# Waits tile by tile, gate functions behind the cells, and attention output reloaded earlier, in a hybrid mLSTM and attention layer

## The chip, the cores and the metric

The kernel runs on one core of one Trainium2 chip. The metric is the device time of one execution in microseconds (us). A core has a matrix engine (PE, with its weight loads PEld), a vector engine (DVE), a scalar engine (ACT), a general engine (POOL), and a sync engine (SP) that mostly issues transfers between the chip's memory (DRAM) and the core's own memory (SBUF). The engines run side by side, each through its own list in order, and wait for each other through semaphores. PE writes to eight banks of a small memory (PSUM), which DVE and ACT empty.

## The reference, cut to what matters

One layer works on 640 tokens (512 latent tokens and 128 context tokens) of width 1024:

```python
hh = rmsnorm(x, g[0]) * (1 + m[1]) + m[0];  x = x + 0.5 * m[2] * swiglu(hh, w1, w3, w2)
hh = rmsnorm(x, g[1]) * (1 + m[4]) + m[3];  x = x + m[5] * token_mixer(hh)
hh = rmsnorm(x, g[2]) * (1 + m[7]) + m[6];  x = x + 0.5 * m[8] * swiglu(hh, w1, w3, w2)
# token_mixer:
att = diff_attention(...)            # 8 heads: softmax_0 - lam * softmax_1, times values
hm  = rmsnorm(h_forward + h_backward) * sigmoid(mo)      # 4 heads of a chunked mLSTM
y   = sigmoid(gm) * (hm @ w_br_m) + sigmoid(gd) * (att @ w_br_d);   out = y @ w_out
```

The modulation m is `silu(c) @ w_ada + b`, 9216 numbers for each of two conditions. The mLSTM runs over five chunks of 128 tokens (four latent, one context) forward and backward; every step multiplies the chunk's masked scores with its values, adds the query times the state C, and updates C. All of it is float32: a product is made of three products of split halves (high times high, high times low, low times high).

## The kernel before, in words

**Tiles and stages.** Features lie on the 128 partitions. The stages follow one another: first feed-forward (to about 480 us), projections and the eight attention heads (to about 1085), the four mLSTM heads (to about 1250), the two branch products and the output product (to about 1440), second feed-forward. A weight granule of 1 MB is loaded into one of two `raw` buffers, copied by ACT to its high half (`wH`, L123) and subtracted by DVE to its low half (`wL`); two granules are held split. A unit is 24 matrix products of one granule into one PSUM bank, with an evacuation behind it.

**Filling.** `Fill` holds a list of granules of projections that nothing waits for at once (gates, values, queries of later heads). Between the steps of a head, `fill.slot` puts some of their units into PE's list, so that PE has work while DVE and ACT make the softmax or the next state. `prefetch` splits the next granule ahead.

**The order of the work.** PE's list is in the order in which the code is written (`keep_in_program_order` in `mm` and `tr`). The lists of the other engines are made by a planner, which simulates the program and takes what is ready first, in the order of the code where several are ready. `tc.issue_after(ins)` adds an edge that puts the instructions of a block behind `ins` in their engine's list, without a wait for its end.

**Memory and waits.** Tiles come from pools; a pool's tiles with the same tag share its buffers. When a pool takes over memory of a pool that was closed, the default is that its tiles wait for the whole old pool; with `reuse_waits="tile"` each waits only for the old tiles whose memory it covers. Some pools of the first and last stages have this before the change, the pools of attention (`att`, `ps2`, `ps2s`), of mLSTM (`ml`, `ps3`) and of the branch products (`ps4`, `tmp`, `yy`, `gate`, `out`) do not.

**Around the hand-over.** The last attention head ends with `finish_norm`, the rest of the fill list, and `finish` (L1324 on), which turns its output into `aT` through two banks and stores it to `aT_dram`. Then the pools of the mLSTM stage open, `csil` and `mask` are loaded, and `Memory.load` (L1580) loads the values (`va`, L1583) and the row maxima (`P`, L1588) of the first head and adds the mask to P on DVE; `load_c` loads both states C. `prep` makes a chunk's token-major keys and scores, `cell` one step in one direction, `gate` (L1662) the output gate `so` by two ACT functions (L1665, L1666), `finish` (L1676) the norm, the gate and the turn back. While head h runs its ten cells, the five preparations of head h+1 and the five finishes of head h-1 are spread over them (`later`).

**Columns.** `Columns` makes the last 24 tiles of the modulation (L683): 512 KB of `w_ada` per tile, two passes of DVE over 1024 columns, one per condition. In the mLSTM stage and beside the branch products their data lie in the `raw` buffers, which the weights use too. `attended` reloads the attention output for the branch product, three pairs at a time through `raw`, and splits it; `drain_beside_columns` runs the branch units, with one column tile to two units.

## Time and profile before

| what | value |
|---|---|
| median of three runs | 1884.49 us (1882.04 to 1887.07) |
| the profiled execution's own time | 1881.62 us |
| its span, first to last instruction | 1879.8 us |
| granted PE clock, mean over the span | 0.986 |
| busy: PE, DVE, ACT, POOL | 97%, 69%, 45%, 2% |
| transfers | 299.82 MB, mean 159 GB/s |

The profile is one execution. Busy is the share of the span in which an engine worked on something; waits are idle time just before an instruction, put down to what came last ("ACT aT L1331" is the instruction of line 1331 that writes the tile aT). "issue" is idle time for which the profile shows no releaser. PEclk is the share of full speed that PE's clock was granted. A row of the timeline has start, duration, engine, line, operation, out<-in, shapes, count, and in brackets the idle time before it. SPq and POOLq rows are the issuing of transfers, not the transfers.

### The profile page before, as it was taken

Reading aid. Unit: us, or ns where it says so; the run is one execution under the profiler, and the core shown is the slowest. Engines: PE = TensorE matmul, PEld = TensorE weight load, DVE = VectorE, ACT = ScalarE, POOL = GpSimd, SP = SyncE. Lnnn points to the kernel's source line nnn. Section 1 sums busy time; section 2 is a strip of 40 time slices with the busy share of each in tenths; the row PEclk is TensorE's granted clock in tenths of the full one; section 3 lists DMA queues with packets and bytes.
Section 4 is the critical chain, followed back from the end, with each engine's and each line's share of the span. In section 5 each row is a group of like instructions: output and inputs, shape, how many; then the busy total and the mean of one; then the engine's idle time right before and its main releaser. Section 6 shows DMA issues by size and latency. Waiting matters only on the chain.

```text
span 1879.8 us, 30792 instructions
## 1 busy us (share of the span) xinstructions
PE 1814.6 (97%) x12658; PEld 1777.6 (95%) x12658; DVE 1292.9 (69%) x2179; ACT 851.3 (45%) x1459; POOL 35.3 (2%) x57
## 2 busy tenths in 40 slices
PE   6999999999999999999999989999899899999989
PEld 4999999999999999999999978899899899999989
DVE  7888886575787655755745467757757778886575
ACT  5644554112653443544544355662326455554232
POOL 1000001110000000000000000000000000000000
PEclk9999999999999999999999989999999899999989
DMA  8344448863343221221322264655742444557852
GB/s 327 120 167 156 157 150 323 313 218 119 123 151 128 72 96 55 77 101 46 104 74 74 88 209 153 208 183 185 255 158 75 151 146 166 188 181 270 328 196 90
DMA packets 127438, 299.82 MB, mean 159 GB/s; under 512 B 9473, under 2 KB 90625, under 8 KB 114625
## 3 DMA queue, kind: packets, MB, share of 16 engines
q1 hardware_dynamic: 118642, 259.07, 39.7%
q0 software_dynamic: 8656, 38.80, 5.6%
q8 instruction: 99, 1.62, 0.4%
q14 instruction: 41, 0.34, 0.1%
HBM read 234.20 MB, written 63.63 MB: 158 GB/s over the span
## 4 chain that ended last, share of the span: by engine, by line
PE 83%; DVE 7%; DMA 6%; ACT 3%; issue 1%; SPq 0%; DVEq 0%; ACTq 0%
PE ps_f L52 42%; PE ps_p L52 18%; PE ps_t L52 11%; DMA raw_a<-in_w_ada_c 2%; PE sc L52 2%; PE ps_o L52 2%; PE ps_n L52 2%; DMA ada<-csil_dram 2%; PE ps_wT L55 1%; PE ps_u L52 1%; PE ps_qkT L55 1%; DVE raw_a L683 1%; DVE junk L683 1%; DMA x<-in_x 1%; DMA P<-nm_dram 0%
## 5 line engine op out<-in xcount | busy, mean ns | idle before, releaser
L52 PE MATMUL ps_f<-S,ww 128*128 128x320 f32 x1992 | 319.7, 310 | 4.5 <-ACT ww L279 2.7
L52 PEld LDWEIGHTS ps_f<-S,ww 128*128 128x128 f32 x1992 | 300.4, 189 | 5.0 <-ACT ww L279 3.0
L52 PE MATMUL ps_p<-hH,wH 128*128 128x320 f32 x864 | 275.0, 318 | 9.5 <-DVE y L39 5.1
L52 PE MATMUL ps_p<-hH,wL 128*128 128x320 f32 x864 | 268.3, 311 | 0.0
L52 PE MATMUL ps_p<-hL,wH 128*128 128x320 f32 x864 | 268.2, 310 | 0.0
L52 PE MATMUL ps_f<-hm,ww 128*128 128x320 f32 x1248 | 201.5, 314 | 8.8 <-ACT ww L279 5.6
L52 PEld LDWEIGHTS ps_f<-hm,ww 128*128 128x128 f32 x1248 | 190.8, 192 | 10.2 <-ACT ww L279 5.9
L52 PE MATMUL ps_t<-wH,hH 128*128 128x256 f32 x640 | 185.1, 289 | 0.9 <-ACT nt L207 0.9
L52 PE MATMUL ps_t<-wH,hL 128*128 128x256 f32 x640 | 181.5, 284 | 0.9 <-DVE hL L39 0.9
L52 PE MATMUL ps_t<-wL,hH 128*128 128x256 f32 x640 | 181.3, 283 | 0.0
L39 DVE TENSOR_TENSOR ww<-raw,ww 128x2048 fp32r<-128x2048 f32 (+1 forms) x62 | 138.8, 2238 | 55.9 <-ACT ww L279 42.2
L52 PEld LDWEIGHTS ps_p<-hH,wH 128*128 128x128 f32 x864 | 163.7, 189 | 11.2 <-issue 5.3
L52 PEld LDWEIGHTS ps_p<-hL,wH 128*128 128x128 f32 x864 | 163.6, 189 | 0.5
L52 PEld LDWEIGHTS ps_p<-hH,wL 128*128 128x128 f32 x864 | 163.4, 189 | 0.0
L52 PE MATMUL ps_f<-hm,wB 128*128 128x320 f32 x1008 | 161.5, 309 | 0.0
L52 PEld LDWEIGHTS ps_f<-hm,wB 128*128 128x128 f32 x1008 | 151.3, 188 | 0.0
L279 ACT ACTIVATE ww<-raw 128x2048 fp32r<-128x2048 f32 x48 | 91.8, 1912 | 104.8 <-DVE raw L39 53.8
L39 DVE TENSOR_TENSOR wL<-raw,wH 128x2048 fp32r<-128x2048 f32 x49 | 112.0, 2287 | 37.4 <-ACT wH L123 37.4
L123 ACT ACTIVATE wH<-raw 128x2048 fp32r<-128x2048 f32 x49 | 93.6, 1910 | 91.2 <-PE ps_p L52 53.3
L39 DVE TENSOR_TENSOR raw<-raw 128x1024 f32<-128x1024 f32 (+1 forms) x144 | 123.9, 862 | 1.4
L52 PEld LDWEIGHTS ps_t<-wH,hH 128*128 128x128 f32 x640 | 123.0, 192 | 1.3 <-ACT nt L207 1.1
L52 PEld LDWEIGHTS ps_t<-wH,hL 128*128 128x128 f32 x640 | 122.8, 192 | 1.1 <-DVE hL L39 1.1
(298 smaller groups left out, 3231.5 us busy)
## 6 DMA issues: line engine op xcount, KB each, us to landing
g_dram<-g SPq DMA_DIRECT2D x44, 640.0 KB, 3.9
raw_a<-in_w_ada_c SPq DMA_DIRECT2D x32, 512.0 KB, 4.1
raw<-in_w1b SPq DMA_DIRECT2D x11, 1024.0 KB, 4.8
raw<-in_w3b SPq DMA_DIRECT2D x11, 1024.0 KB, 4.8
raw<-in_w1a SPq DMA_DIRECT2D x10, 1024.0 KB, 4.8
raw<-in_w3a SPq DMA_DIRECT2D x10, 1024.0 KB, 4.9
hm<-g_dram POOLq DMA_DIRECT2D x8, 1280.0 KB, 10.2
raw_a<-in_w_ada_k SPq DMA_DIRECT2D x8, 1024.0 KB, 8.4
```

The costliest lines, as they stand in the source:

```text
L39: return eng.tensor_tensor(out=out, in0=in0, in1=in1, op=op)
L52: tc.keep_in_program_order(nc.tensor.matmul(*args, **kw))
L55: tc.keep_in_program_order(nc.tensor.transpose(*args, **kw))
L123: act(h, raw, AF.Copy)
L279: act(t[0], flat, AF.Copy)
L683: vec.tensor_tensor_reduce(out=junk, in0=raw, in1=self.csil[:, v, :], op0=ALU.mult, op1=ALU.add, scale=1.0, scalar=0.0, accum_out=mod[:, c ...
```

## The change

There are three groups of edits. Pools of attention, mLSTM and the later stages get `reuse_waits="tile"`, and with it some tiles move: the last head's transposes go to the score banks, the first mLSTM head's mask, va, P and C are loaded by POOL's queue, `y1` is taken pair by pair, column data leave `raw` (after nine tiles) for the tiles `so`/`N` and then `k3`/`k2`, and two of the four x loads come behind the columns. The gate's two functions, the mask sums and the column passes are put behind named instructions of the cells; the gate of the last head comes after the fifth cell and lies in `q2`. The eight `attended` calls start at the last head's first cell.

```diff
         def fetch(self, ahead=0):
-            while len(self.next) < min(ahead or self.ahead, self.n):
+            while len(self.next) < min(ahead or self.ahead, self.n, len(self.todo)):
...
-    ap = att.enter_context(tc.tile_pool(name="att", bufs=1))
-    psum = att.enter_context(tc.tile_pool(name="ps2", bufs=5, space=PSUM))
-    ps_s = att.enter_context(tc.tile_pool(name="ps2s", bufs=1, space=PSUM))
+    ap = att.enter_context(tc.tile_pool(name="att", bufs=1, reuse_waits="tile"))
+    psum = att.enter_context(tc.tile_pool(name="ps2", bufs=5, space=PSUM, reuse_waits="tile"))
+    ps_s = att.enter_context(tc.tile_pool(name="ps2s", bufs=1, space=PSUM, reuse_waits="tile"))
...
+            if self.hd == 7:
+                last = ps_s.tile([128, 1536], F32, tag="sc", name="ps_aT")
             for i0, n in ((0, 4), (4, 1)):
-                p = psum.tile([128, 4, 128], F32, tag="mm", name="ps_aT")
+                if self.hd < 7:
+                    p = psum.tile([128, 4, 128], F32, tag="mm", name="ps_aT")
+                else:
+                    p = last[:, i0 * 128 : (i0 + 4) * 128].rearrange("p (a b) -> p a b", a=4)
...
     (k_pool, q_pool, cs_p, mp, ps3, and later ps4, tmp, yy, gate, out: the same reuse_waits="tile")
-    mask = load(mp, [128, 2, 128], a["mask"], name="mask")
+    mask = mp.tile([128, 2, 128], F32, name="mask")
+    nc.gpsimd.dma_start(out=mask, in_=a["mask"])
...
-        def load(self):
+        def load(self, behind=None):
             h = self.h
+            queue = nc.sync if h else nc.gpsimd
-            nc.sync.dma_start(out=self.va[:, :, 0:256], in_=v_dram[h])
+            queue.dma_start(out=self.va[:, :, 0:256], in_=v_dram[h])
...
-                nc.sync.dma_start(
+                queue.dma_start(
                     out=self.P[:, :, d, :], in_=nm_dram[32 * d + h]...
                 )
-                tt(vec, self.P[:, :, d, :], self.P[:, :, d, :], mask[...], ALU.add)
+                with ExitStack() as st:
+                    if behind is not None:
+                        st.enter_context(tc.issue_after(behind.ins))
+                    tt(vec, self.P[:, :, d, :], self.P[:, :, d, :], mask[...], ALU.add)
...
         def load_c(self):
-            self.C = [load(mp, [128, 2, 258], a["c_aug"][d, self.h], tag=f"C{d}", name="C", bufs=2) for d in range(2)]
+            self.C = [mp.tile([128, 2, 258], F32, tag=f"C{d}", name="C", bufs=2) for d in range(2)]
+            for d in range(2):
+                (nc.sync if self.h else nc.gpsimd).dma_start(out=self.C[d], in_=a["c_aug"][d, self.h])
...
         (prep, cell: self.at_prep, self.at_act, self.at_vec are the last score product on DVE, the
          copy wv on ACT, and the last DVE step of a cell)
         def gate(self):
-            self.so = load(mp, [128, 2, T], o_dram[:, 2 * h : 2 * h + 2, :], tag="so", name="so")
-            act(self.so, self.so, AF.Ln, bias=1.0)
-            act(self.so, self.so, AF.Exp, scale=-1.0)
+            self.so = mp.tile([128, 2, T], F32, tag="so", name="so") if h < 3 else pair("q", 2, "so")
+            dma(self.so, o_dram[:, 2 * h : 2 * h + 2, :])
+            with tc.issue_after(self.at_act.ins):
+                act(self.so, self.so, AF.Ln, bias=1.0)
+                act(self.so, self.so, AF.Exp, scale=-1.0)
...
-            mem[h + 1].load()
+            mem[h + 1].load(mem[h].at_prep)
...
             for k in range(KT):
-                later[2 + k].append(attended)
-        later[9].append(m.gate)
+                later[k].append(attended)
+        later[9 if h < 3 else 4].append(m.gate)
...
-            if len(box_ml) % 4 == 0:
+            if len(box_ml) % 4 == 0 and len(box_ml) < 36:
                 columns.fetch(1)
-            elif len(box_ml) % 4 == 2:
-                columns.tile()
+            elif len(box_ml) % 4 == 2 and len(box_ml) < 36:
+                columns.tile(m.at_vec)
...
-    y1 = pairs("q", "y1")
+    y1 = {}     # y1[g] = pair("q", g, "y1") at the first evacuation of granule g
...
+    def load_columns(src):
+        t = mp.tile([128, 2, T], F32, tag="so", name="raw_a").rearrange("p a t -> p (a t)")[:, :D]
+        dma(t, src)
+        return t, mp.tile([128, 2, 258], F32, tag="N", name="junk")...
+    columns.load, columns.ahead = load_columns, 1
+    columns.fetch()
     for i in range(5):
         fill.one()
         mem[3].finish(i)
-        columns.fetch((i + 1) % 2)
         if i % 2:
-            columns.tile()
+            columns.tile(box["y"])
...
     def drain_beside_columns():
         n = 0
         while fill.q:
-            columns.fetch((n + 1) % 2)
             fill.one()
             if n % 2 and columns.n:
-                columns.tile()
+                columns.tile(box["y"])
             n += 1
+    columns.n, n_left = columns.n - 8, 8
     drain_beside_columns()
...
-    x_pairs = pairs("k", "x")
+    x_pairs = [pair("k", i, "x") for i in range(2)]
+    (load_columns now takes k3 for the data and k2 for the scratch output)
+    columns.load, columns.n = load_columns, n_left
+    columns.fetch()
...
-        for g in range(4):
+        for g in range(2):
             nc.sync.dma_start(out=x_pairs[g], in_=x_dram[:, 2 * g : 2 * g + 2, :])
         drain_beside_columns()
     cs.close()
+    x_pairs += [pair("k", i, "x") for i in range(2, 4)]
+    for g in range(2, 4):
+        nc.sync.dma_start(out=x_pairs[g], in_=x_dram[:, 2 * g : 2 * g + 2, :])
```

`box["y"]` is the last DVE step of the latest branch evacuation.

## The prediction

> **What bounds the kernel now.** I read the page first (busy shares, then the chain that ended last), then busy time by stretch, then the waits of TensorE (PE) in the stretch that the change rewrites, and last the timelines around each wait.

> ```profile
> span 1879.8 us, 30792 instructions
> PE 1814.6 (97%) x12658; PEld 1777.6 (95%) x12658; DVE 1292.9 (69%) x2179; ACT 851.3 (45%) x1459; POOL 35.3 (2%) x57
> ...
> PE 83%; DVE 7%; DMA 6%; ACT 3%; issue 1%; SPq 0%; DVEq 0%; ACTq 0%
> ```

> PE is busy for 97% of the span and makes 83% of the chain. No matrix product is removed, so only PE's idle time and its slow clock can be won. Where are they?

> ```profile
> 600.00:1066.00 466.00, 460.91 (x3598) 454.49 (x3597) 274.70 (x445) 210.90 (x407) 0.00 (x0) 1.00 0.24 80
> 1066.00:1100.00 34.00, 28.78 (x197) 28.33 (x195) 15.44 (x30) 13.14 (x32) 0.00 (x0) 0.95 0.53 166
> 1248.00:1322.00 74.00, 68.44 (x466) 67.75 (x464) 47.14 (x89) 32.09 (x49) 0.00 (x0) 1.00 0.62 219
> 1322.00:1416.00 94.00, 94.00 (x629) 93.76 (x629) 59.03 (x100) 29.40 (x38) 0.00 (x0) 0.98 0.53 187
> ```

> The columns are the stretch, then busy PE, weight load, DVE, ACT and POOL, granted clock, DMA share, GB/s. The attention heads (600 to 1066 us) leave 5.1 us idle in 466. The 34 us in which attention hands over to the mLSTM heads leave 5.2, the end of the mLSTM stage 5.6 in 74, the mLSTM branch products 0. PE's own waits from 1050 to 1460 us:

> ```profile
> PE ps_p L52 <- DVE y L39: 5.1, 1, 5.1
> PE ps_n L52 <- issue: 3.7, 1, 3.7
> PE ps_p L52 <- ACT aT L1331: 2.5, 1, 2.5
> PE ps_n L52 <- ACT stage L1404: 1.4, 1, 1.4
> PE ps_p L52 <- ACT num L1631: 1.1, 1, 1.1
> PE ps_n L52 <- ACT Cn L1647: 0.8, 1, 0.8
> PE ps_p L52 <- DVE wL L39: 0.5, 1, 0.5
> ```

> These seven sum to 15.1 us. A gap also costs clock after it:

> ```profile
> 546.00 7.03 PE ps_p L52 x48
> ...
> 1085.08 8.84 PE ps_p L52 x48
> ```
> ```profile
> 1086.30:1089.70 3.40, 3.40 (x15) 3.40 (x14) 0.15 (x4) 0.00 (x0) 0.00 (x0) 0.50 0.79 218
> 1100.00:1106.80 6.80, 5.84 (x14) 4.64 (x15) 4.34 (x10) 4.35 (x15) 0.00 (x0) 0.50 1.09 368
> 1321.80:1325.20 3.40, 3.25 (x12) 3.28 (x13) 2.29 (x2) 0.90 (x1) 0.00 (x0) 0.50 1.01 422
> ```

> The first pair is from the chain in order of time: 48 products take 7.03 us, or 8.84 behind the 2.5 us gap. Three stretches at clock 0.50 follow the three largest gaps: half of 3.4, 6.8 and 3.4 us is 6.8 us. So 15.1 + 6.8 = 21.9 us is all that these waits can give back.

> **The change, part by part.** *Hand-over, first wait (2.5 us).* Every tile of the old mLSTM pools waits for the whole attention pool, so the first product waits for the copy aT of the last head, which runs on ACT right behind this one:

> ```profile
> 1083.77 0.42 ACT L1404 ACTIVATE stage<-ps_p 128x320 f32<-128x320 f32 x1
> ```

> Tile by tile it waits only for the last reader of its own bank, and the last head's transposes now sit in the score banks. At best that reader is long done and 2.5 goes. At worst it is the quoted copy, which ends at 1084.2, and PE starts 0.9 us before today's 1085.08. I take 1.6, between them.

> *Hand-over, second wait (3.7 us).* The page calls it "issue"; the timelines show who is late:

> ```profile
> 1087.23 1.40 SPq L1554 DMA_DIRECT2D csil<-csil_dram  x2
> ...
> 1089.15 0.54 SPq L1583 DMA_DIRECT2D va<-v_dram  x1
> 1089.73 2.08 SPq L1588 DMA_DIRECT2D P<-nm_dram  x2
> 1091.86 3.00 SPq L74 DMA_DIRECT2D C<-in_c_aug  x2
> ```
> ```profile
> 1092.91 1.23 DVE L683 CUSTOM_DVE_ANT_0 raw_a<-raw_a,csil 128x1024 bf16<-128x1024 f32 x1 [5.34 <-DMA csil<-csil_dram]
> ...
> 1097.68 0.83 DVE L39 TENSOR_TENSOR P<-P,mask 128x640 f32<-128x640 f32 x1
> ...
> 1100.43 1.75 DVE L39 TENSOR_TENSOR P<-ps_st,P 128x256 f32<-128x256 f32 x5 [0.95 <-ACT P L1612]
> ```

> No load is issued before the attention pool is free at about 1087. P leaves at 1089.73, its mask is added at 1097.68, behind four column passes (the quoted one is the first), and the first of its five products is made from 1100.43 on; PE starts its first cell when that is done, half a us later. The change moves six transfers of the first head (mask, va, two P, two C) from SP to POOL, which does nothing here, and lets each wait for its own memory only; without the mask 0.54 + 2.08 + 3.00 = 5.6 us of issuing leave SP's queue, and nothing stands behind them on POOL until the last feed-forward. The column passes are put behind the cell's DVE work. If P's memory is that of tiles which the last head is done with ahead of its closing norm, P leaves near 1080, lands 8 us later and is ready near 1091. PE, which reaches the first cell at about 1094 (1101 less 3.7, 1.6 and 1.7), no longer waits: 3.7. If its memory comes free no earlier than the last attention store, or POOL is slow, it is 0. POOL's issues of this shape are not in the trace; the nearest rows are these:

> ```profile
> hm<-g_dram POOLq DMA_DIRECT2D x8, 1280.0 KB, 10.2
> P<-nm_dram SPq DMA_DIRECT2D x8, 320.0 KB, 8.1
> hm<-g_dram SPq DMA_DIRECT2D x2, 1280.0 KB, 13.4
> raw_a<-in_w_ada_c SPq DMA_DIRECT2D x32, 512.0 KB, 4.1
> x<-x_dram SPq DMA_DIRECT2D x8, 640.0 KB, 6.0
> ```

> The same 1280 KB land in 10.2 us from POOL and 13.4 from SP, so I take 3.7 whole. [...]

> *Slow clock after both.* 3.4/2 + 6.8/2 = 5.1 us at most, 0 at least. I take 3.0: the first stretch may stay if some gap stays, and in the second PE would in part have waited for the cells' ACT and DVE steps anyway. [...]

> *End of the mLSTM stage (5.1 + 0.5 us and the slow clock).* The wait is put down to a DVE product, but DVE was done with it; the weights are late too:

> ```profile
> 1293.65 16.25 SPq L74 DMA_DIRECT2D raw_a<-in_w_ada_c  x4
> 1312.34 3.88 SPq L74 DMA_DIRECT2D raw<-in_w_brm  x2
> 1317.17 1.91 ACT L123 ACTIVATE wH<-raw 128x2048 fp32r<-128x2048 f32 x1 [17.63 <-DMA raw<-in_w_brm]
> 1319.11 2.29 DVE L39 TENSOR_TENSOR wL<-raw,wH 128x2048 fp32r<-128x2048 f32 x1 [2.45 <-ACT wH L123]
> ```

> Four modulation columns sit in the two raw buffers from 1293 to 1312, so the branch weights are asked for at 1312.34, split from 1317.17 on, and the low half is done at 1319.11 + 2.29 = 1321.4, where PE restarts. The change gives these columns the tiles of the gate and of the state, later of k3 and k2. Raw is then free by about 1300, and 4.8 us of load (1312.34 to 1317.17) with 4.2 of splitting end before 1312, ahead of PE's need at about 1316.5. The pool wait on the DVE product goes too. I take 5.1 + 0.5 + 1.7 = 7.3; at least 0, if the load still comes late.

> *Cells (1.4 + 1.1 + 0.8 us).* The rows show ACT doing long things ahead of short ones that PE waits for:

> ```profile
> 1145.89 1.56 ACT L1612 ACTIVATE P<-P,cols 128x128 f32<-128x128 f32 x5
> 1147.35 0.46 ACT L1631 ACTIVATE num<-ps_n,cols 128x258 f32<-128x258 f32 x1
> ...
> 1192.72 1.25 ACT L1666 ACTIVATE so<-so 128x1280 f32<-128x1280 f32 x1
> ```

> The gate's two functions (1.25 us each) now follow the cell's last ACT step, and the next head's two mask sums (0.83) follow the last preparation. These are orders, not new waits on data, but whatever lands late there still holds up the copies behind it. The last gate moves from after the tenth cell to after the fifth, with its 640 KB load, and to the tile q2; the eight attention pairs with their three loads come two cells earlier, on SP and in raw. The sum is 3.3; I take 2.0, bounds 0 and 3.3.

> *Covered parts.* Fifteen of the 24 column tiles change their buffer and keep their two passes of 1.23 us. Eight now run beside the sixteen branch units, one per two units (7.03 us): 1.23 + 1.23 + 4.1 for the single-buffered load is 6.6, so it fits; DVE has 35 of 94 us free there. Two of the four x loads follow the last of these tiles. They land about 2.5 + 6 us behind the sixteenth unit and the first output units that need them have eight banks, 28 us, to wait in: 0, or a loss if that cover is gone (third rival).

> *Charge for the new order.* Waits per tile change what each queue carries, and the planner reorders three engines over 400 us. Its stalls today are 0.8 to 1.4 us each; I charge three, 4.0 us, bounds 0 and 8. Sum: 1.6 + 3.7 + 3.0 + 7.3 + 2.0 - 4.0 = 13.6 us. The profiled execution took 1881.62 us (1.8 around its span) and the median is 1884.49, 2.9 above. 1881.6 - 13.6 + 2.9 = 1870.9, so 1871.

> **The rivals.** *The loads of the first head stay late:* P's tile lies on memory that is freed last, or POOL is slow. Then the 3.7 and the 3.0 stay lost and the gain is 13.6 - 6.7 = 6.9: 1877.6. For it: nothing in the trace shows POOL with a transfer of many short rows. Against: POOL is empty here. [...]

> *The stalls form again elsewhere:* the charge reaches the sum; three short waits today came from ACT work put early, and the attention pairs at ACT are now put earlier still. About 1884, no change.

> *The columns chain becomes late (slower).* With one buffer, each of the eight tiles needs its load, two passes and the next issue inside 7.03 us. Should loads take 10.4 us instead of 4.1, as the second feed-forward's weights do:

> ```profile
> raw<-in_w2b SPq DMA_DIRECT2D x8, 384.0 KB, 10.4
> ```

> then eight tiles of 10.4 + 2.5 = 12.9 us last 103 us, 47 past the sixteenth unit, and x lands at 53. PE has run eight units, 28 us, ahead by then: 25 us lost, less the 13.6, makes 1884.5 + 11 = 1896. It decides from a landing of about 7 us, where eight tiles take 76 us. Against: the median is 4.1.

> *All comes back with no charge:* 21.9 us, and up to 1863.

> **How the numbers follow.** About 0.3%, 5.6 us, is what a measurement of this kernel can tell from no change: faster means under 1878.8. Forecast 0.47 and full gain 0.12, both faster. Late loads 0.15, of which 0.11 fall under 1878.8. Stalls again 0.15, of which 0.13 within and 0.02 slower. Late columns or another new wait of that size 0.11, slower. Together faster 0.70, same 0.17, slower 0.13. The range: 1861 holds the full gain and a little clock, 1886 the case of no change.

> **What would show it.** Right: PE's idle in the hand-over falls from 5.2 to under 2 us, no P add stands behind a column pass, POOL carries six more transfers near 1075 us; the load of the branch weights is issued before 1305 and PE has no gap over 1 us between stage and branch products. Wrong: the first P product still follows a load; new waits of PE on ACT num, Cn or stage over 2 us; DVE waiting for raw columns beside the branch units, then PE for x. The prediction falls if the gain sits elsewhere than in these four places, above all in the feed-forwards, which the change does not touch.

## The result and the profile after

The changed kernel takes 1868.26 us (median of five runs, 1864.51 to 1872.94), the kernel before 1884.49 beside it: a ratio of 0.9916, with a 95% interval of 0.9903 to 0.9930. The forecast was 1871. The profiled execution took 1865.82 us. Its page begins:

```profile
span 1864.0 us, 30788 instructions
PE 1807.2 (97%) x12658; PEld 1770.8 (95%) x12658; DVE 1295.9 (70%) x2179; ACT 847.7 (45%) x1456; POOL 39.7 (2%) x63
...
PE 84%; DVE 7%; DMA 5%; ACT 2%; issue 1%; SPq 0%; DVEq 0%; ACTq 0%
```

PE runs the same 12658 products, POOL has six more instructions, and the span is 15.8 us shorter. PE's waits from 1050 to 1460 us, largest first (three short waits of the second feed-forward are left out):

```profile
PE ps_n L52 <- issue: 3.1, 1, 3.1
PE ps_aT L55 <- ACT aT L1336: 2.3, 1, 2.3
PE ps_n L52 <- DVE C L42: 1.5, 1, 1.5
PE ps_p L52 <- DVE C L42: 0.5, 1, 0.5
PE ps_n L52 <- ACT Cn L1659: 0.5, 1, 0.5
```

The 5.1 us for y, and the waits for stage, num and wL, are gone. The two waits of the hand-over are not: 3.7 on "issue" became 3.1, and 2.5 for aT became 2.3 in front of another instruction. Busy time by stretch, with the columns of the prediction's table:

```profile
1066.00:1100.00 34.00, 28.60 (x206) 28.09 (x205) 12.26 (x27) 15.32 (x37) 2.85 (x4) 1.00 0.60 190
...
1240.00:1400.00 160.00, 160.00 (x1091) 159.67 (x1090) 113.61 (x204) 57.52 (x84) 0.00 (x0) 1.00 0.62 222
```

From 1240 to 1400 PE does not pause at all. In the hand-over it is idle for 5.4 of 34 us, as long as before (5.2), but the granted clock is 1.00 instead of 0.95.

To set kernels side by side I cut each trace at four products of PE: the last head's first transpose (ps_aT), the first cell's first product (ps_n), the last cell's last product (ps_u), and the first product of the norm behind the output product (ps_ss). The stretches are the hand-over, the cells, and the end of the mLSTM stage with the branch and output products. Each number is a difference of two start times in us, from one profiled execution. The ratio is to the kernel before, measured beside each. The labels are those of the experiments below.

| kernel | hand-over | cells | end and branches | sum | median, us | ratio [95%] |
|---|---|---|---|---|---|---|
| before | 19.06 | 150.37 | 163.71 | 333.1 | 1884.49 | |
| after | 16.69 | 146.39 | 156.17 | 319.3 | 1868.26 | 0.9916 [0.9903, 0.9930] |
| e1 columns in raw | 18.22 | 147.29 | 192.55 | 358.1 | 1906.72 | 1.0117 [1.0103, 1.0131] |
| e2 pools whole | 22.33 | 148.31 | 157.52 | 328.2 | 1875.91 | 0.9953 [0.9939, 0.9966] |
| e3 turn first | 16.04 | 147.37 | 156.17 | 319.6 | 1866.02 | 0.9910 [0.9896, 0.9924] |
| e4 turn, exp first | 14.06 | 147.12 | 156.17 | 317.4 | 1865.26 | 0.9898 [0.9885, 0.9912] |
| e5 loads on SP | 20.38 | 149.71 | 156.17 | 326.3 | 1873.72 | 0.9952 [0.9937, 0.9967] |
| e6 gate back | 23.58 | 148.92 | 156.17 | 328.7 | 1875.12 | 0.9961 [0.9947, 0.9975] |
| e7 reload back | 16.69 | 148.29 | 156.17 | 321.2 | 1870.04 | 0.9927 [0.9905, 0.9949] |
| e8 raw, no holds | 16.68 | 147.77 | 165.45 | 329.9 | 1876.52 | 0.9971 [0.9959, 0.9983] |
| e9 next bank | 14.05 | 146.23 | 156.20 | 316.5 | 1865.26 | 0.9900 [0.9883, 0.9917] |
| e10 no holds | 16.68 | 146.58 | 156.17 | 319.4 | 1867.77 | 0.9914 [0.9899, 0.9930] |
| e11 pools alone | 20.14 | 150.11 | 163.41 | 333.7 | 1881.24 | 0.9988 [0.9975, 1.0002] |
| e12 after again | 16.69 | 147.66 | 156.20 | 320.6 | 1869.56 | 0.9922 [0.9905, 0.9938] |

Before to after the three stretches give 2.4 + 4.0 + 7.5 = 13.9 us. The rest of the span gives some 2 us. That is scatter: the trace of e7 has the same instructions in the same order on every engine as the changed kernel, as has e12, and the rest of the span took 1544.7 us in the changed kernel, 1541.8 in e7 and 1546.8 in e12 (1546.7 before).

What happens in the hand-over shows in its timelines. PE, then POOL, then DVE, ACT and DVE again, of the changed kernel:

```profile
1085.30 0.33 PE L55 MATMUL ps_aT<-ident,ao 128*128 128x128 f32 x1 [2.32 <-ACT aT L1336]
...
1072.31 1.73 POOL L1595 DMA_DIRECT2D P<-nm_dram  x2 [57.41 <-ACT wT L1301]
...
1086.63 0.82 DVE L39 TENSOR_TENSOR P<-P,mask 128x640 f32<-128x640 f32 x1
...
1095.86 0.90 ACT L1647 ACTIVATE wv<-va,cols 128x258 f32<-128x258 f32 x2
1096.66 3.02 ACT L1624 ACTIVATE P<-P,cols 128x128 f32<-128x128 f32 x10
...
1098.54 1.75 DVE L39 TENSOR_TENSOR P<-ps_st,P 128x256 f32<-128x256 f32 x5 [10.35 <-ACT P L1624]
```

The first wait moved: the fifth transpose now shares a score tile with the first four and waits for their copy. P's loads leave at 1072.31 (1089.73 before) and the mask is added at 1086.63 (1097.68 before). But ACT makes the ten exponentials of P only at 1096.66, in its list behind the copies of the keys and wv, so DVE stands 10.35 us and PE 3.1.

### The profile page after: what moved, and what is told of

It is laid out like the page before. It is cut to its first block, busy times and chain, and to the rows that moved or that the text cites. A ratio compares the mean times of both kernels' runs of the same rounds, so it can differ in the third digit from the quotient of the medians.

```text
span 1864.0 us, 30788 instructions
## 1 busy us (share of the span) xinstructions
PE 1807.2 (97%) x12658; PEld 1770.8 (95%) x12658; DVE 1295.9 (70%) x2179; ACT 847.7 (45%) x1456; POOL 39.7 (2%) x63
## 4 chain that ended last, share of the span: by engine, by line
PE 84%; DVE 7%; DMA 5%; ACT 2%; issue 1%; SPq 0%; DVEq 0%; ACTq 0%
PE ps_f L52 41%; PE ps_p L52 21%; PE ps_t L52 11%; PE sc L52 2%; PE ps_o L52 2%; PE ps_n L52 2%; DMA raw_a<-in_w_ada_c 2%; DMA ada<-csil_dram 2%; PE ps_u L52 1%; PE ps_wT L55 1%; PE ps_qkT L55 1%; DVE junk L683 1%; DVE raw L39 1%; DMA hm<-g_dram 1%; DMA x<-in_x 1%
## 5 line engine op out<-in xcount | busy, mean ns | idle before, releaser
L52 PE MATMUL ps_f<-S,ww 128*128 128x320 f32 x1992 | 319.4, 310 | 4.3 <-ACT ww L279 2.7
L52 PEld LDWEIGHTS ps_f<-S,ww 128*128 128x128 f32 x1992 | 299.7, 188 | 5.0 <-ACT ww L279 3.0
L52 PE MATMUL ps_p<-hH,wH 128*128 128x320 f32 x864 | 273.5, 317 | 1.2 <-DVE mkT L1464 0.7
L52 PE MATMUL ps_p<-hH,wL 128*128 128x320 f32 x864 | 267.0, 309 | 0.0
L52 PE MATMUL ps_p<-hL,wH 128*128 128x320 f32 x864 | 266.8, 309 | 0.0
L52 PE MATMUL ps_f<-hm,ww 128*128 128x320 f32 x1248 | 199.6, 312 | 9.2 <-ACT ww L279 5.6
L52 PEld LDWEIGHTS ps_f<-hm,ww 128*128 128x128 f32 x1248 | 189.2, 191 | 10.4 <-ACT ww L279 5.9
L52 PE MATMUL ps_t<-wH,hH 128*128 128x256 f32 x640 | 185.2, 289 | 0.0
L52 PE MATMUL ps_t<-wH,hL 128*128 128x256 f32 x640 | 181.8, 284 | 1.1 <-DVE hL L39 1.1
L52 PE MATMUL ps_t<-wL,hH 128*128 128x256 f32 x640 | 181.6, 284 | 0.0
L39 DVE TENSOR_TENSOR ww<-raw,ww 128x2048 fp32r<-128x2048 f32 (+1 forms) x62 | 138.8, 2239 | 55.1 <-ACT ww L279 40.4
L52 PEld LDWEIGHTS ps_p<-hH,wH 128*128 128x128 f32 x864 | 162.4, 188 | 2.3 <-DVE C L42 0.9
L52 PEld LDWEIGHTS ps_p<-hL,wH 128*128 128x128 f32 x864 | 162.4, 188 | 0.5
L52 PEld LDWEIGHTS ps_p<-hH,wL 128*128 128x128 f32 x864 | 162.2, 188 | 0.0
L52 PE MATMUL ps_f<-hm,wB 128*128 128x320 f32 x1008 | 161.5, 309 | 0.0
L52 PEld LDWEIGHTS ps_f<-hm,wB 128*128 128x128 f32 x1008 | 151.3, 188 | 0.0
L39 DVE TENSOR_TENSOR wL<-raw,wH 128x2048 fp32r<-128x2048 f32 x49 | 112.1, 2287 | 37.2 <-ACT wH L123 37.2
L123 ACT ACTIVATE wH<-raw 128x2048 fp32r<-128x2048 f32 x49 | 93.6, 1911 | 81.9 <-PE ps_p L52 71.1
L39 DVE TENSOR_TENSOR raw<-raw 128x1024 f32<-128x1024 f32 (+1 forms) x144 | 124.2, 864 | 1.4
L52 PEld LDWEIGHTS ps_t<-wH,hL 128*128 128x128 f32 x640 | 123.1, 192 | 1.6 <-DVE hL L39 1.5
L52 PEld LDWEIGHTS ps_t<-wL,hH 128*128 128x128 f32 x640 | 123.3, 193 | 0.2
## 6 DMA issues: line engine op xcount, KB each, us to landing
raw_a<-in_w_ada_c SPq DMA_DIRECT2D x32, 512.0 KB, 4.0
hm<-g_dram POOLq DMA_DIRECT2D x8, 1280.0 KB, 9.7
```

Of the source, the lines that this page charges most:

```text
L39: return eng.tensor_tensor(out=out, in0=in0, in1=in1, op=op)
L52: tc.keep_in_program_order(nc.tensor.matmul(*args, **kw))
L123: act(h, raw, AF.Copy)
```

## The experiments

**e1: the column data back in raw.** All else is the changed kernel; the holds behind `box["y"]` stay.

```diff
-    columns.load, columns.ahead = load_columns, 1     # tiles so / N
-    columns.fetch()
+        columns.fetch((i + 1) % 2)                    # beside the finishes
+            columns.fetch((n + 1) % 2)                # beside the branch units
-    columns.load, columns.n = load_columns, n_left    # tiles k3 / k2
-    columns.fetch()
+    columns.n = n_left
```

> The changed kernel with one part undone: the last 15 column tiles use the two raw buffers again, with the fetches of before. Theory A (the branch weights were late because columns held raw): PE's wait ahead of the branch products comes back with 4 to 6 us and the time rises by 5 to 9 us over the changed kernel, to a ratio of about 0.995 to 0.997 to the kernel before. Theory B (the pool wait on the DVE product made that wait, as the wait list of before names it): the wait stays away, the ratio stays near 0.9916.

Measured: 1.0117 [1.0103, 1.0131], 38 us above the changed kernel and slower than the one before, far outside of what either theory said. PE's two longest waits from 1240 to 1420 us, and SP's queue:

```profile
PE ps_p L52 <- ACT wH L123: 19.2, 3, 10.5
PE ps_p L52 <- DVE wL L39: 6.9, 5, 1.9
```
```profile
1297.43 17.98 SPq L74 DMA_DIRECT2D raw_a<-in_w_ada_c  x4
...
1322.12 0.33 SPq L74 DMA_DIRECT2D raw<-in_w_brm  x1
```

In the changed kernel SP issues the same load here:

```profile
1278.85 0.33 SPq L74 DMA_DIRECT2D raw<-in_w_brm  x1
```

26.1 us of waiting for split weights. Four columns hold raw, and the first `w_brm` granule is asked for at 1322.12. The end of the stage is 36.4 us longer than in the changed kernel; most of the rest is clock: 30.7 us of that stretch were at half clock, with PE busy in 15.8 of them, which is some 8 us by my estimate. The rival of a late columns chain is real, then, but it sits at the weights behind the columns, not at x. Whether raw alone does it, or raw with the holds, e8 separates.

**e2: pools that wait whole.** Every engine's list stays that of the changed kernel; only waits differ.

```diff
-    ap = att.enter_context(tc.tile_pool(name="att", bufs=1, reuse_waits="tile"))
+    ap = att.enter_context(tc.tile_pool(name="att", bufs=1))
     # likewise ps2, ps2s, mlk, mlq, csil, ml, ps3, ps4, tmp, yy, gate, out
```

> The changed kernel with the waits per tile taken back in the thirteen pools that the change touched; every engine's list of instructions is the same, so only waits differ. Theory A: PE's wait ahead of the branch products stays at 1 to 2 us (only the last evacuation's DVE product is waited for), while in the hand-over POOL's loads leave only after the last attention store, near 1088 us, and PE's wait for the first cell grows from 3.1 to 5 to 8 us; together 4 to 8 us over the changed kernel, ratio 0.994 to 0.996. Theory B: the branch wait returns with about 5 us besides, ratio 0.997 or more. A third view, that waits per tile matter nowhere: ratio 0.9916.

Measured: 0.9953 [0.9939, 0.9966]. PE's four longest waits from 1066 to 1420 us, and POOL's first issues:

```profile
PE ps_n L52 <- DVE P L39: 6.5, 1, 6.5
PE ps_aT L55 <- ACT aT L1336: 2.3, 1, 2.3
PE ps_n L52 <- DVE C L42: 1.2, 1, 1.2
PE ps_p L52 <- DVE y L39: 1.1, 1, 1.1
```
```profile
1090.80 0.54 POOL L1572 DMA_DIRECT2D mask<-in_mask  x1 [591.99 <-DVE va L1592]
1091.34 0.88 POOL L1590 DMA_DIRECT2D va<-v_dram  x1
1092.21 1.74 POOL L1595 DMA_DIRECT2D P<-nm_dram  x2
```

POOL is empty, yet P leaves at 1092.21: it waits for the whole attention pool. The hand-over is 5.6 us longer than in the changed kernel; 3.9 of that is idle time of PE (9.25 us against 5.40), the other 1.7 a stretch of 3.4 us at half clock. At the branches 1.4 us come back (the wait for y). The cells are 1.9 us longer, but that shows nothing: executions with the lists of the changed kernel took from 146.39 to 148.29 us there.

**e3: the five transposes ahead of their two copies.**

```diff
             for i0, n in ((0, 4), (4, 1)):
                 ...  tr(p[:, i, :], self.ao[:, i0 + i, :], ident)
+                parts.append((i0, n, p))
+            for i0, n, p in parts:
                 act(aT[:, i0 * 128 : (i0 + n) * 128], ...)
```

> The changed kernel with one edit: the five transposes of the last attention head's output come before the two copies that empty them, instead of four, copy, one, copy. If the 2.3 us wait in front of the fifth transpose is a wait on the shared score tile, it goes and the time falls by 1 to 3 us (ratio about 0.990 to 0.991); PE's next wait there is then for the bank of the first product, under 1 us. If something else was late there (a semaphore that also covers the first product), the gap reappears one instruction later and the time stays.

Measured: 0.9910 [0.9896, 0.9924], which is not to be told from the changed kernel; the hand-over is 0.65 us shorter. The wait moves on by one instruction:

```profile
PE ps_n L52 <- issue: 3.1, 1, 3.1
PE ps_p L52 <- ACT stage L1412: 1.6, 1, 1.6
```

These are e3's two longest waits from 1066 to 1240 us. The first product of the mLSTM stage now stands 1.6 us for the copy stage, which ACT makes behind wH: the bound that the prediction named. I had expected under 1 us here.

**e4: e3, and the ten exponentials ahead of the key copies on ACT.**

```diff
+    for i in range(5):
+        mem[0].exps(i)          # the exponentials, out of prep
...
+                if h == 0:
+                    st.enter_context(tc.issue_after(self.at_exp.ins))
                 act(self.ktok[:, i, :], p[:, 0:256], AF.Copy)
```

> As the kernel with the transposes first, and the ten exponentials of the first mLSTM head's P are put ahead of its five preparations on ACT. If PE's remaining 3.1 us ahead of the first cell is ACT's order (P's sums were done at 1088 us, its exponentials started at 1096.7), that wait falls under 1 us and the time by 2 to 4 us against the kernel with transposes first: ratio about 0.988 to 0.990. If P's data or the score products are late instead, the wait stays at 3 us and the ratio equals that of the other kernel.

Measured: 0.9898 [0.9885, 0.9912]. The 3.1 us on "issue" are gone (the three longest waits from 1066 to 1240 us):

```profile
PE ps_p L52 <- ACT stage L1412: 1.6, 1, 1.6
PE ps_n L52 <- DVE C L42: 1.5, 1, 1.5
PE ps_k L55 <- DVE P L39: 0.9, 1, 0.9
```

So what was late in the changed kernel is the order of ACT's list, and 2.0 us of hand-over come back by it (16.04 to 14.06). The whole kernel's median falls by 0.8 us against e3, less than the 2 to 4 expected and less than these intervals can tell.

**e5: the first head's loads on SP.**

```diff
-            queue = nc.sync if h else nc.gpsimd
+            queue = nc.sync
```

(the same for C and the mask)

> The six transfers of the first mLSTM head (mask, va, two P, two C) go back from POOL to SP; all else is the changed kernel. Theory A (ScalarE's order is late, not the load): in the changed kernel P leaves at 1072.31 us and its mask is added at 1086.6, but ScalarE makes the exponentials only at 1096.66, behind five copies of mktok and two wv. From SP the loads may leave up to 14 us later and are still in time; the wait ahead of the first cell stays at 3.1 us or grows by less than 1, ratio to the kernel before 0.991 to 0.9925. Theory B (the queue is what was won, as the prediction has it): P's loads fall behind other loads on SP as before, the wait grows from 3.1 to 5 us or more and stretches at half clock come back in the hand-over: 4 to 7 us slower than the changed kernel, ratio 0.9935 to 0.9955.

Measured: 0.9952 [0.9937, 0.9967]: theory B. SP's queue, DVE, and PE's longest wait from 1066 to 1240 us:

```profile
1072.58 14.16 SPq L1410 DMA_DIRECT2D gm_dram<-stage  x4
1087.79 0.32 SPq L1337 DMA_DIRECT2D aT_dram<-aT  x1
...
1092.52 2.24 SPq L1595 DMA_DIRECT2D P<-nm_dram  x2
...
1101.22 0.82 DVE L39 TENSOR_TENSOR P<-P,mask 128x640 f32<-128x640 f32 x1 [12.77 <-DMA P<-nm_dram]
```
```profile
PE ps_n L52 <- DVE P L39: 6.8, 1, 6.8
```

The memory is as free as in the changed kernel, but on SP the loads stand behind four stores of stage and the store of aT, which wait for copies that are made as late as 1087, and then behind four other loads. Counted from the last head's first transpose, P leaves 18.5 us later than from POOL (1092.52 less 1084.11, against 1072.31 less 1082.38). ACT's order alone made 3.1 us late; the queue would make it 6.8.

**e6: the gate's functions not held, the last gate after the tenth cell.**

```diff
-            with tc.issue_after(self.at_act.ins):
-                act(self.so, self.so, AF.Ln, bias=1.0)
-                act(self.so, self.so, AF.Exp, scale=-1.0)
+            act(self.so, self.so, AF.Ln, bias=1.0)
+            act(self.so, self.so, AF.Exp, scale=-1.0)
...
-        later[9 if h < 3 else 4].append(m.gate)
+        later[9].append(m.gate)
```

> The gate's two functions are no longer held behind the cell's last step on ScalarE, and the last head's gate is made after its tenth cell again; all else is the changed kernel. Theory A (the cells' gain is this order's): TensorE's waits on num, Cn and stage among the cells come back, 1 to 3 us between 1105 and 1240, ratio 0.9918 to 0.9932. Theory B (the cells' 1.3 us came with the pools or with the clock): 0.9905 to 0.9918, and no wait on num, Cn or stage over 1 us.

Measured: 0.9961 [0.9947, 0.9975], slower than either theory had it, and in another place. ACT's list in the hand-over, and PE's longest wait from 1066 to 1240 us:

```profile
1094.50 0.90 ACT L1647 ACTIVATE wv<-va,cols 128x258 f32<-128x258 f32 x2
1099.72 1.27 ACT L1678 ACTIVATE so<-so 128x1280 f32<-128x1280 f32 x1 [4.32 <-DMA so<-o_dram]
1101.02 1.27 ACT L1679 ACTIVATE so<-so 128x1280 f32<-128x1280 f32 x1
1102.20 3.01 ACT L1624 ACTIVATE P<-P,cols 128x128 f32<-128x128 f32 x10
```
```profile
PE ps_n L52 <- issue: 10.0, 1, 10.0
```

Without the hold the planner puts the first head's gate ahead of the exponentials. ACT stands 4.32 us for the gate's load, then works 2.5 on it, while ten ready exponentials wait behind: 6.9 us more hand-over. Among the cells no wait on num, Cn or stage comes back (0.3 us in all), so the later last gate shows in no wait. The hold matters at the first cell of the first head.

**e7: the attention output reloaded from the third cell on.**

```diff
-                later[k].append(attended)
+                later[2 + k].append(attended)
```

> The attention output is reloaded from the last head's third cell on again, not from its first; all else is the changed kernel. Theory A (the reload was hidden where it was): no wait over 1 us is added, ratio 0.9905 to 0.9922. Theory B (its three loads share the two raw buffers with the branch weights, so two cells later they make the first branch weights late): a wait on wH or on the attention pairs of 2 us or more ahead of the branch products, ratio 0.9925 to 0.994.

Measured: 0.9927 [0.9905, 0.9949]. PE's only waits of 1 us or more from 1050 to 1420 us are those of the changed kernel (3.1, 2.3, and 1.3 for C), and the end takes the same 156.17 us. The traces say why: each engine's instructions stand in the same order as in the changed kernel. The planner puts the reload in the same places from either point of the code, so this part of the change changes nothing, and e7 is one more measurement of the changed kernel.

**e8: e1 without the holds.** `columns.tile()` for `columns.tile(box["y"])` beside the branch units.

> As the first run: the modulation columns beside the branch units stay in the two raw buffers, and besides they are no longer held behind the unit's own product on VectorE. Theory A (in the first run it was the hold that kept the buffers: 1906.7 us, with 26 us of TensorE waiting for wH and wL): without the hold the columns leave the buffers as early as in the kernel before, waits for wH and wL beside the branch units come to 2 to 8 us, ratio 0.994 to 0.998. Theory B (the two buffers shared by fifteen columns and the branch weights cost this by themselves, once the columns start as late as in the changed kernel): waits of 15 us or more stay, ratio 1.004 or more.

Measured: 0.9971 [0.9959, 0.9983]: theory A. The end takes 165.45 us, nearly as before the change (163.71). PE's two longest waits from 1240 to 1420 us:

```profile
PE ps_p L52 <- DVE wL L39: 3.0, 2, 1.8
PE ps_p L52 <- ACT wH L123: 2.3, 1, 2.3
```

Raw alone costs 165.45 - 156.17 = 9.3 us; the holds make 27.1 more of it (192.55 - 165.45). As I read it, a column that waits for a branch evacuation keeps the buffer of the weights which that branch needs next.

**e9: e4, and the first PSUM bank skipped.**

```diff
     psum = ml.enter_context(tc.tile_pool(name="ps3", bufs=8, space=PSUM, reuse_waits="tile"))
+    psum.tile([128, 512], F32, tag="mm", name="ps_skip")
```

> As the fourth run (five transposes of the last head ahead of their two copies, the ten exponentials of the first head's P ahead of its copies on ScalarE), and besides the first tile of the mLSTM's banks is skipped, so that the first product after the transposes takes a bank that was read longer ago. Theory A (that product waits for the copy stage that reads its own bank: 1.6 us in the fourth run): the wait falls under 0.5, ratio to the kernel before 0.988 to 0.9895. Theory B (it waits for something else that ends at the same time, or the next instruction then waits for its own copy): the wait moves on, ratio 0.9893 to 0.991.

Measured: 0.9900 [0.9883, 0.9917]; the wait of 1.6 us for stage is still there, and the hand-over unchanged (14.05). But this does not test theory A. The tile that nothing writes took no bank here: the programs of e4 and e9 are the same, with every instruction, bank and wait, and the traces have the same order on every engine. In both, the first product behind the transposes writes the very bank that the copy stage reads. So the wait fits theory A, which no run tests, and e9 is a second measurement of e4.

**e10: the changed kernel without the holds beside the branches.** The edit of e8, made to the changed kernel.

> The changed kernel, but the column passes beside the branch units are not held behind the unit's product on VectorE; the columns keep their own tiles. Theory A (with tiles of their own no weight stands behind a column, so the hold costs and gains nothing there): no wait of TensorE over 1 us between 1240 and 1400, ratio 0.990 to 0.9925, as the changed kernel. Theory B (the hold is part of the gain: without it column passes stand ahead of a weight split or of a product's evacuation): waits on wL or y of 2 us or more come back, ratio 0.9935 or more.

Measured: 0.9914 [0.9899, 0.9930], with 156.17 us at the end: theory A. With tiles of their own for the columns the holds neither cost nor gain. With e1 and e8 this makes all four cases: the holds cost 27.1 us where the columns lie in raw, and nothing where they do not.

**e11: the kernel before, with pools that wait tile by tile.** The edit of e2 the other way round, made to the kernel before; every engine's list stays as it was.

> The kernel before with nothing changed but that its thirteen pools wait tile by tile. Every engine's list is that of the kernel before. Theory A (the pools give little by themselves: P's loads still stand on SP behind stores of stage, and raw still holds the columns): the waits on issue, stage and raw stay, only the 2.5 us for aT and part of the 5.1 us for y can go, ratio 0.996 to 1.000. Theory B (the pools carry the hand-over whatever the queue): P's loads leave early, ratio 0.9935 to 0.9955.

Measured: 0.9988 [0.9975, 1.0002], no change that can be told: theory A. PE's waits from 1066 to 1420 us begin so:

```profile
PE ps_n L52 <- DVE P L39: 7.2, 1, 7.2
PE ps_p L52 <- DVE wL L39: 2.8, 2, 1.8
PE ps_p L52 <- ACT wH L123: 2.1, 1, 2.1
PE ps_p L52 <- ACT stage L1404: 1.6, 1, 1.6
```

PE passes the old waits for aT and y sooner and loses the same time at P and at the weights.

**e12: the changed kernel once more**, beside e9 to e11.

> The changed kernel once more, beside the others on the same chip: ratio 0.990 to 0.993 by either theory; its interval is what the variants with small gains are set against.

Measured: 0.9922 [0.9905, 0.9938]. e4 and e9, which are one program, are 4.3 us faster than e12 by the medians and 3.0 faster than the first measurement of the changed kernel. Their intervals overlap those of the changed kernel, so a gain of 3 to 4 us is likely and not settled.

## Why the prediction was right, and where its steps were not

The forecast was 13.6 us of gain; the three stretches gave 13.9, and the medians 16.2. The size is right with terms that are partly wrong, and that they add up is partly luck. With the same program the three stretches gave 11.9 us in e7 and 12.5 in e12; the difference is mostly clock (below). One sign that I had named for being right did not come: PE's idle time in the hand-over was to fall from 5.2 to under 2 us, and is 5.4.

- **Hand-over, first wait: 1.6 predicted, 0.2 measured.** That tile by tile the first product "waits only for the last reader of its own bank" fits: e3 shows it behind the copy stage, the worse of my two cases, with 1.6 us. The step that failed is what stands ahead of it. I overlooked that the change puts both groups of transposes into one score tile, so the fifth waits 2.3 us for the copy of the first four.
- **Hand-over, second wait: 3.7 predicted, 0.6 measured.** The half on the loads holds: P left at 1072.31 and was ready ahead of 1091, as said. That PE "no longer waits" there failed, because I followed the load and not ACT's list, where the exponentials stand behind the copies; e4 shows this. The step is still needed: whole pools (e2) or SP's queue (e5) make the hand-over longer than before the change, 22.33 and 20.38 us against 19.06. P's two loads from POOL landed 4.8 us after their issue (median).
- **Slow clock: 3.0 predicted.** The stretch at 1086.30 in the hand-over cost half of 3.4, 1.7 us; of the second PE ran from 1100.96 to 1106.80, which cost 2.9. All 4.6 are gone in the profile. In e12 one stretch of 3.4 us stays, 2.9 of it in the cells (1.4 us), so 3.2 came back there; in e7 one of 6.8 stays, 5.9 of it in the cells (2.9 us), so 1.7 came back. The size was about right by luck: the gaps are still there, and where they fell on the clock's grid decided (below).
- **End of the mLSTM stage: 7.3 predicted, 7.5 measured**, by the step as it was put. Weights are asked for at 1278.85, PE has no gap, and e8 loses 9.3 us when the columns return to raw.
- **Cells: 2.0 predicted, charge for the new order -4.0.** The waits for stage, num and Cn fell from 3.5 to 0.5 us (with one of 0.2 that the list ahead leaves out), 3.0 gained; new waits for C cost 2.0 (1.5 + 0.5). Together +1.0 where I had -2.0: the charge was twice what new waits cost. The cells' 4.0 us fit: 2.9 of clock and 1.1 of waits. Where the prediction counts the gate's order under the cells alone, the step failed: e6 shows that it protects the hand-over, with 6.9 us there. The earlier reload, counted here too, is nothing (e7).
- **Covered parts: 0 predicted.** PE waits nowhere for x or weights from 1240 to 1400 us, and e10 agrees by its time.

Ahead of the longer wait for C, DVE stood with the next head's mask sum, one of the steps that the change moved:

```profile
1176.13 0.83 DVE L39 TENSOR_TENSOR P<-P,mask 128x640 f32<-128x640 f32 x1 [3.43 <-DMA P<-nm_dram]
```

Its load was late, the updates of C follow in DVE's list, and PE waits for one of them until 1180.18. Four steps of a finish also stand between those updates; no run separates the two.

The two hand-over waits came out 4.5 us short; the clock (1.6 more than forecast) and the cells with the charge (3.0 more) made up for it in this profile. The rival "the loads of the first head stay late" is what e5 and e2 make true (1873.7 and 1875.9, predicted 1877.6). "The columns chain becomes late" did not come with the columns' own tiles. A late chain did come in e1, in the raw buffers, by another path than I had described: through the weights and not through x, at 38 us.

## What to carry to other kernels

A stall at a hand-over may need several conditions at once: memory that is free, a queue that is not blocked, and an engine whose list has the work early. Here each of three edits, taken away alone, made the hand-over longer than in the old kernel, and one of them put in alone gained nothing; follow the late value through load, queue and every engine's list before pricing one link. A hold that orders work behind a consumer cost nothing here where the held work had its own buffer, and 27 us where it kept a buffer that the consumer's next input needed. And an edit can leave the program as it was: two of the experiments did (e7 and e9), so compare every engine's list before reading a time.

## What the runs showed of the hardware

```profile
1082.89:1086.30 3.41, 1.22 (x8) 1.22 (x9) 2.29 (x1) 2.13 (x4) 0.00 (x0) 1.00 0.27 103
1086.30:1089.71 3.41, 3.41 (x15) 3.41 (x14) 0.15 (x4) 0.00 (x0) 0.00 (x0) 0.50 0.79 219
```
```profile
1080.55:1083.97 3.42, 2.43 (x18) 2.18 (x16) 0.00 (x0) 1.54 (x1) 0.00 (x0) 1.00 0.08 30
1083.97:1087.38 3.41, 2.08 (x15) 2.08 (x16) 3.01 (x7) 1.64 (x4) 0.55 (x1) 1.00 0.28 107
1094.21:1097.62 3.41, 1.78 (x16) 1.58 (x15) 0.00 (x0) 2.81 (x9) 0.00 (x0) 1.00 1.10 339
1097.62:1101.03 3.41, 1.96 (x9) 1.77 (x10) 2.49 (x7) 2.06 (x8) 0.00 (x0) 1.00 1.05 361
```
```profile
1097.08:1100.49 3.41, 0.86 (x8) 0.67 (x7) 0.00 (x1) 3.13 (x11) 0.00 (x0) 1.00 1.16 320
1100.49:1103.90 3.41, 2.88 (x7) 2.36 (x8) 3.21 (x7) 2.03 (x8) 0.00 (x0) 0.50 0.77 298
```
```profile
1092.73:1096.14 3.41, 1.28 (x12) 1.09 (x10) 0.00 (x0) 2.92 (x9) 0.00 (x0) 1.00 1.14 338
1096.14:1102.97 6.83, 5.88 (x14) 4.71 (x15) 4.84 (x12) 5.35 (x18) 0.00 (x0) 0.50 0.46 166
```

Before, PE was idle for 2.19 of 3.41 us in one window (64%), and the next ran at half clock. In the changed kernel's profile both gaps were cut by the grid, into 0.99 and 1.33 us and into 1.63 and 1.45: full clock. In e12 the same second gap put 2.55 us (75%) into one window, and the next was at half; in e7 it put 2.13 us (62%) into one, and the next two were at half. Among the windows of this grid between 1078 and 1108 us in the fourteen profiles, the 14 that began at full clock and were idle for 58% or more were all followed by half clock, and none below that; over the rest of the spans, windows idle for 34 to 55% went either way.

**This is also where the scatter comes from, in part.** The work ahead of the last head's transposes is the same in the changed kernel and in e12, yet the first transpose starts at 1082.38 us in the one and 1084.33 in the other. Ahead of it the trace of the one has 10.2 us at half clock and the other 13.7; half of the difference is 1.7 of these 1.95 us, if PE was busy all through.
